# A decoder block on one core: the first two heads' k and q loaded at the end of the first part of the values' projection

## The chip, the core and the metric

The kernel runs on one core of a Trainium2 chip. The core has five engines that run side by side, each through its own instructions in order: TensorE (PE in the profile, with its weight loads as PEld), VectorE (DVE), ScalarE (ACT), GpSimd (POOL) and SyncE (SP), which here issues nearly all DMA transfers. They wait for each other through semaphores only. The metric is the time of one execution in microseconds (us), as the median of several runs. Lower is better.

## The reference

One transformer block on 1024 tokens of 1024 channels, in float32:

```python
h = rms_norm(x, g_pre_mix[l])
z = h @ w_in[l]
q, k, v, glu_in, z_ga, z_gc = jnp.split(z, ...)
y_attn = dilated_attention_mixer(q, k, v, rel_bias_table, w_attn_out[l])
y_conv = conformer_conv_mixer(glu_in, ...)
merged = jax.nn.sigmoid(z_ga) * y_attn + jax.nn.sigmoid(z_gc) * y_conv
x = x + rms_norm(merged @ w_mix_out[l], g_post_mix[l])
h = rms_norm(x, g_pre_ffn[l])
x = x + rms_norm(swiglu_ffn(h, w_ffn_in[l], w_ffn_out[l]), g_post_ffn[l])
```

The attention has 24 heads of 64 channels, in three groups of eight with dilations 1, 4 and 16. A query sees 128 steps of its dilation backwards, with a bias that depends on the distance. The three groups' outputs are merged per head slot, weighted by their softmax denominators. The convolution is causal and depthwise over 31 taps; a layer norm over the channels and a swish follow it.

## The kernel before

Float32 operands are split in a high and a low half, written as `fp32r`, and a product is made of two or three matmuls of these halves. The kernel is written out by hand: what Python calls in order is the order of each engine's queue.

**The order of the work.** Gated projections, gates and then all q and k are projected (`qk_pair`); k and q of each pair of heads are stored to DRAM. Then comes the stage around the change, the values' projection: six parts (`B.v`, L943, called at L1588), one for each of three groups and two halves of the heads. A part has eight columns of 128 tokens. A column is eight pairs of matmuls, L966 (128x512) and L967 (128x256), into one of six PSUM banks; then ScalarE copies the bank into half of the tile `vsum` (L977), and after every second column GpSimd adds the two halves of the tile up (L988). After columns 3 and 7 two stores take the sums to DRAM (L951 or L953), put five ticks later.

**Ticks.** Side work is spread over the matmuls by a counter. `tick` (L121) is called after every second pair of matmuls of the values' projection, so a column is 4 ticks and a part 32. A tick first does what `later` (L118) has planned for it, then, at every fourth tick, one weight piece, then one step of each background generator. I count ticks from the start of the first part.

**Weights of the parts.** A part has two raw tiles of weights, cut into four pieces. At tick 4 of a part the next part's raw tiles are asked for (L177), at tick 16 its pieces are queued, and at ticks 16, 20, 24 and 28 one piece each is made by ScalarE (cast, L201) and VectorE (subtraction, L202) into a tile of its own. These pieces are for the next part. Each of a part's four weight tiles is last used in its column 7, ticks 29 to 32.

**The convolution's norm** (`conv_norm`, L1294) runs as a background generator through the same ticks. It loads eight tiles of the convolution's output (L1301, four at the start, four at ticks 7 to 18), takes the mean off (L1318, VectorE), squares into a new tile (L1321, ScalarE) and adds the squares up (L1324, VectorE): seven additions, the last at tick 39. At tick 46 TensorE sums over the channels in sixteen small matmuls (L415), ScalarE and VectorE make the reciprocal root of it (L419 to L424), and at tick 53 TensorE spreads it over the partitions (L430). Then each of the eight tiles is scaled (L1336) and put through the swish (L1339).

**The attention** (`attention`, L999) is a generator of its own. Its first `next` calls `stack_load` five times, which loads k and q of the first two heads: two tiles for q's high and low halves of each head (L892, L893), one tile for k of each head (two loads each, L899) and the bias tile (L488): nine DMA issues on SP's queue and six tiles. It also plans two calls of `double` (L904), in each of which GpSimd copies half of q's columns from one half of the partitions to the other (L908, L909, four copies). Then it does nothing until `normed` is 9, which the norm sets at tick 83. From the end of the first part on it is stepped by `beat`, 2.52 times a tick. Its first products are the scores, L1082.

**Buffers.** The tiles of 128x1024 called `b` come from one pool of 42 (`NSLOT`, `slot`, L80): normalised input, weights, raw weights, convolution tiles, squares and the heads' k and q alike. When a new tile is asked for and none is free, the instruction that first writes it waits for the last use of the one that it takes over.

Of the kernel before, what the change touches and what calls it, by code (L numbers as in the profile page):

```python
# [62 lines left out]
class Build:  # L63
# [935 lines left out]
    def attention(self):  # L999

        live, s, total = {}, 0, 96
        order = [(g, 2 * hg + i) for hg in range(2) for g in range(3) for i in range(2)]
        nxt, cur, u, x, V = self.stacks(*order.pop(0)), None, 8, None, None
        for i in range(5):
            self.stack_load(nxt)
        for hf in range(2):
            self.later(22 + 5 * hf, lambda p=nxt, hf=hf: self.double(p, hf))
        second = self.stacks(*order.pop(0))

        def there():  # L1010
            return nxt[1] // 2 * 3 + nxt[0] < self.vn

        while s < total + self.LP:
            if s < total:
                if x is None and nxt and there():
                    x = self.values(*nxt[:2])
                if u == 8:
                    while self.normed < 9 or x is None:
                        if second and second[5] < min(5, self.normed - 6):
                            self.stack_load(second)  # L1020
                        if x is None and there():
                            x = self.values(*nxt[:2])
                        yield 0
                    cur, u, nxt, V = nxt, 0, None, []
                    self.ending = s == total - 8
                live[s] = a = {}
                self.att_s(a, cur, V, u)
                u += 1

                if u in (4, 5):  # L1030
                    if len(V) < 2:
                        V.append(self.value_parts(x, u - 4))
                    if u == 5:
                        x = None
                if u == 6 and cur[0] == 2:
                    self.other_stats(cur)
                if u in (6, 7) and nxt:
                    self.double(nxt, u - 6)
                if u == 8:
                    cur[2] = cur[3] = V = None  # L1040
                if u == 1:
                    if second:
                        nxt, second = second, None
                    elif order:
                        nxt = self.stacks(*order.pop(0))
                if nxt and nxt[5] < 5:
                    self.stack_load(nxt)
            if 0 <= s - 1 < total:
                self.att_e(live[s - 1])
            yield 0  # L1050
            done, self.added = self.added, None
            if done:
                next(done)
            if 0 <= s - self.LT < total:
                self.att_t(live, s - self.LT)
                yield 0
            for _ in done or ():
                pass
            done = None
            if 0 <= s - self.LP < total:  # L1060
                yield from self.att_p(live, s - self.LP)
            s += 1
        for _ in self.added:
            pass
        self.added = None
# [381 lines left out]
def build(ctx, tc, aps):  # L1447
    B = Build(ctx, tc, aps)
# [133 lines left out]
    att = B.attention()  # L1582

    B.vsum = B.slot()
    vs = list(vj.values()) + [late[:1] or co[:1]]
    B.later(20, lambda: next(att))
    for i, (g, hg) in enumerate(vj):
        B.v(g, hg, vs[i], vs[i + 1])  # L1588
        if i == 0:
            B.fine = att  # L1590
        elif i == 4:
            assert cn not in B.gens
            cs = []
            B.later(16, lambda: cs.append(B.bg(B.conv_split())))
# [18 lines left out]
    def gate_load(d, late=0):  # L1613
        c = B.slot()
        if late:
            B.later(late, lambda: nc.sync.dma_start(c, d))
        else:
            nc.sync.dma_start(c, d)
        return c

    nxt = gate_load(B.d_gc[0], 1)
    ws = {}

    for n, hf in [(n, hf) for hf in range(2) for n in range(3)] + [(n, hf) for n in range(3, 8) for hf in range(2)]:
        if hf == 0:
            ws[n] = B.weights(co[n])
            mg[n] = nxt
            nxt = gate_load(B.d_gc[n + 1]) if n < 7 else (gate_load(B.d_ga[0]), gate_load(B.d_gc[0]))
# [221 lines left out]
    for j in range(PLAIN, FT):  # L1850
        s = [None, None]
        p, odd = divmod(j, 2)
# [231 lines left out]
```

## Time and profile before

| | us |
|---|---|
| median of 3 runs | 1693.77 |
| lowest and highest run | 1693.01, 1693.94 |
| the profiled execution, its own time | 1696.67 |
| its span, first to last instruction | 1694.9 |
| TensorE busy | 1679.5 (99%) |
| VectorE busy | 1260.1 (74%) |
| ScalarE busy | 817.2 (48%) |
| GpSimd busy | 511.4 (30%) |
| first pair of the values' projection (L966) | at 549.4 |
| first scores of the attention (L1082) | at 620.0 |
| HBM traffic | 169 GB/s over the span |

A row of a timeline gives the start, the duration, the engine, the line, the operation, the output and inputs by the program's names, their shapes and a count; in brackets stands the idle time of the engine before it and what ended it. A row of waits names the waiting instruction, what it waited for, the sum in us, how often, and the longest. A row of a window gives, for each engine, the busy time and the count of instructions, then the granted share of TensorE's clock, the busy share of the DMA engines and the GB/s. TensorE's matmuls overlap, so their durations do not add up; the distance of their starts tells the rate.

### The profile page before, as it was taken

What the parts mean: (1) busy time and instruction counts of PE and PEld (TensorE: products, weight loads), DVE (VectorE), ACT (ScalarE), POOL (GpSimd) and SP (SyncE); (2) the same over time, 40 slices, a digit from 0 to 9 for tenths busy, and PEclk for the clock granted to TensorE, in tenths of its full rate; (3) what the DMA queues carried; (4) which work ended last, traced back from release to release, by engine and by line L of the source; (5) the groups of instructions that cost most, each with busy time, mean ns of one, the idle gap of its engine ahead of it and who ended that gap; (6) DMA issues with size and microseconds to landing.
All of it is one profiled execution on the core that took longest, in us unless ns stands there. A gap on an engine that the chain in (4) does not pass through costs nothing.

```text
span 1694.9 us, 23464 instructions
## 1 busy us (share of the span) xinstructions
PE 1679.5 (99%) x8167; PEld 1406.3 (83%) x8167; DVE 1260.1 (74%) x2209; ACT 817.2 (48%) x1599; POOL 511.4 (30%) x399
## 2 busy tenths in 40 slices
PE   9999999999999999999999999999999999999998
PEld 7788888888888789999888888888888888888886
DVE  6789988888999668778985845775665566677686
ACT  6344334434444478888812446633333333354453
POOL 0017777887886345665300400000000000000000
PEclk9999999999999999999999999999999999999999
DMA  4342433455566877789998622132223222494334
GB/s 167 113 178 88 149 124 131 149 198 178 170 170 174 267 250 233 221 239 245 323 271 315 218 88 100 44 130 94 93 103 121 94 93 95 174 376 126 107 124 155
DMA packets 162563, 283.36 MB, mean 167 GB/s; under 512 B 47249, under 2 KB 78988, under 8 KB 162444
## 3 DMA queue, kind: packets, MB, share of 16 engines
q1 hardware_dynamic: 161948, 281.42, 50.7%
q8 instruction: 64, 1.05, 0.3%
q14 instruction: 55, 0.45, 0.1%
q0 software_dynamic: 352, 0.18, 0.1%
q10 hardware_dynamic: 144, 0.26, 0.0%
HBM read 191.10 MB, written 95.42 MB: 169 GB/s over the span
## 4 chain that ended last, share of the span: by engine, by line
PE 50%; DMA 1%; ACT 0%; DVE 0%; issue 0%; DVEq 0%
PE p L1968 12%; PE p L336 7%; PE p L334 7%; PE p L335 7%; PE p L1697 5%; PE p L318 3%; PE p L320 3%; PE p L319 3%; DMA b<-dw 1%; PE p L1428 0%; PE p L1153 0%; DVE b L1635 0%; ACT b L1286 0%; PE p L1082 0%; ACT b L1434 0%
## 5 line engine op out<-in xcount | busy, mean ns | idle before, releaser
L334 PE MATMUL p<-b,b 128*128 128x512 f32 x1204 | 468.8, 389 | 0.5 <-ACT c L353 0.3
L335 PE MATMUL p<-b,b 128*128 128x512 f32 x1204 | 468.4, 389 | 0.0
L336 PE MATMUL p<-b,b 128*128 128x512 f32 x1204 | 468.4, 389 | 0.0
L334 PEld LDWEIGHTS p<-b,b 128*128 128x128 f32 x1204 | 226.0, 188 | 48.4 <-DVE c L862 1.0
L335 PEld LDWEIGHTS p<-b,b 128*128 128x128 f32 x1204 | 226.0, 188 | 47.0
L336 PEld LDWEIGHTS p<-b,b 128*128 128x128 f32 x1204 | 226.0, 188 | 47.0
L1968 PE MATMUL p<-b,b 128*128 128x512 f32 x924 | 209.6, 389 | 0.0
L1968 PEld LDWEIGHTS p<-b,b 128*128 128x128 f32 x924 | 173.4, 188 | 36.0
L708 DVE SCALAR_TENSOR_TENSOR p<-b,par,p 128x511 f32<-128x511 f32 (+14 forms) x232 | 163.3, 738 | 0.0
L966 PE MATMUL p<-b,b 128*128 128x512 f32 x384 | 146.2, 412 | 2.1 <-DVE b L202 2.1
L318 PE MATMUL p<-b,b 128*128 128x512 f32 x368 | 147.0, 399 | 0.0
L320 PE MATMUL p<-b,b 128*128 128x512 f32 x368 | 143.6, 390 | 0.0
L319 PE MATMUL p<-b,b 128*128 128x512 f32 x368 | 143.5, 390 | 0.0
L208 ACT CAST b<-d 128x1024 fp32r<-128x1024 f32 x86 | 90.4, 1051 | 105.2 <-POOL d L229 55.2
L209 POOL TENSOR_TENSOR b<-d,b 128x1024 fp32r<-128x1024 f32 x44 | 106.9, 2429 | 79.9 <-ACT b L208 72.5
L209 DVE TENSOR_TENSOR b<-d,b 128x1024 fp32r<-128x1024 f32 x42 | 51.3, 1221 | 101.0 <-ACT b L208 101.0
L1287 DVE TENSOR_TENSOR b<-b,b 128x512 fp32r<-128x512 f32 x133 | 92.4, 699 | 22.0 <-ACT b L1286 20.1
L967 PE MATMUL p<-b,b 128*128 128x256 f32 x384 | 108.6, 283 | 0.0
L1286 ACT CAST b<-b 128x512 fp32r<-128x512 f32 x133 | 82.1, 619 | 48.4 <-PE p L1968 18.7
L1095 ACT ACTIVATE c<-c,stat 128x128 f32<-128x128 f32 (+1 forms) x192 | 85.1, 447 | 13.6 <-DVE stat L1085 12.4
L1697 PE MATMUL p<-b,b 128*128 128x512 f32 x384 | 89.4, 391 | 0.0
L208 ACT CAST b<-b 128x1024 fp32r<-128x1024 f32 x47 | 49.5, 1052 | 77.5 <-POOL b L236 37.2
(233 smaller groups left out, 2913.1 us busy)
## 6 DMA issues: line engine op xcount, KB each, us to landing
b<-w_in SPq DMA_DIRECT2D x30, 512.0 KB, 4.7
dk<-c SPq DMA_DIRECT2D x48, 256.0 KB, 4.4
dq<-c SPq DMA_DIRECT2D x48, 256.0 KB, 3.7
b<-dq SPq DMA_DIRECT2D x48, 256.0 KB, 4.0
b<-dk SPq DMA_DIRECT2D x48, 256.0 KB, 7.8
b<-w_fi SPq DMA_DIRECT2D x24, 512.0 KB, 5.3
d<-w_in SPq DMA_DIRECT2D x23, 512.0 KB, 4.5
dqS<-c SPq DMA_DIRECT2D x44, 256.0 KB, 2.1
```

The source lines that it names most:

```text
L208: self.nc.scalar.copy(hi, x)
L209: self.wsplit.tensor_tensor(lo, x, f(hi), op=OP.subtract)
L318: nc.tensor.matmul(ps, hi[:, s], a, start=kt == 0, stop=False)
L319: nc.tensor.matmul(ps, hi[:, s], b, start=False, stop=False)
L320: nc.tensor.matmul(ps, lo[:, s], a, start=False, stop=kt == nk - 1)
L334: nc.tensor.matmul(ps, hi[:, s], a, start=first and kt == 0, stop=False, skip_group_check=True)
L335: nc.tensor.matmul(ps, hi[:, s], b, start=False, stop=False, skip_group_check=True)
L336: nc.tensor.matmul(ps, lo[:, s], a, start=False, stop=kt == 3, skip_group_check=True)
L708: nc.vector.scalar_tensor_tensor(A[i][:, j:], src[i][:, :H - j], w[i], A[i][:, j:], op0=OP.mult, op1=OP.add)
L966: nc.tensor.matmul(ps, a, w, start=kt == 0, stop=kt == KT - 1, skip_group_check=True)
L1697: nc.tensor.matmul(banks[tt][nh], st, wt[:, nh * H:(nh + 1) * H], start=bool(kt == 0 and a), stop=bool(kt == KT - 1 and b))
L1968: nc.tensor.matmul(acc[t], x, y, start=first and e == 0, stop=last and e == 2, skip_group_check=True)
```

## The change

The attention's first step moves from tick 20, inside the first part, to the end of the first part, tick 32, after all of that part's instructions. The two calls of `double` are planned 17 and 22 ticks after that step in place of 22 and 27, so that they fall on ticks 49 and 54 where they were on 42 and 47. No instruction is added or taken away.

```diff
@@ -1004,7 +1004,7 @@
         for i in range(5):
             self.stack_load(nxt)
         for hf in range(2):
-            self.later(22 + 5 * hf, lambda p=nxt, hf=hf: self.double(p, hf))
+            self.later(17 + 5 * hf, lambda p=nxt, hf=hf: self.double(p, hf))
         second = self.stacks(*order.pop(0))
 
         def there():
@@ -1583,10 +1583,10 @@
 
     B.vsum = B.slot()
     vs = list(vj.values()) + [late[:1] or co[:1]]
-    B.later(20, lambda: next(att))
     for i, (g, hg) in enumerate(vj):
         B.v(g, hg, vs[i], vs[i + 1])
         if i == 0:
+            next(att)
             B.fine = att
         elif i == 4:
             assert cn not in B.gens
```

## The prediction

> **What bounds the kernel now.** I read the page, then TensorE's waits, then windows and timelines around the start of the values' projection.
>
> ```profile
> span 1694.9 us, 23464 instructions
> PE 1679.5 (99%) x8167; PEld 1406.3 (83%) x8167; DVE 1260.1 (74%) x2209; ACT 817.2 (48%) x1599; POOL 511.4 (30%) x399
> ...
> PE p L966 <- DVE b L202: 2.1, 1, 2.1
> PE p L415 <- DVE b L1324: 1.3, 1, 1.3
> PE p L501 <- DVE eps_ln L444: 1.2, 1, 1.2
> ```
>
> TensorE sets the time: it is busy nearly throughout, and all its waits together are a few us. The two longest lie close together, at the start of the stage that the change touches. They are these:
>
> ```profile
> 578.11 0.50 PE L966 MATMUL p<-b,b 128*128 128x512 f32 x1 [2.12 <-DVE b L202]
> 587.31 2.96 PE L415 MATMUL p<-mean_col,b 128*128 128x1 f32 x16 [1.31 <-DVE b L1324]
> 597.27 1.03 PE L430 MATMUL p<-ident,rs 128*128 128x128 f32 x8
> ...
> 32.29 1.84 PE L415 MATMUL p<-mean_col,b 128*128 128x1 f32 x16
> ...
> 584.60:588.00 3.40, 2.09 (x15) 1.65 (x14) 2.55 (x2) 1.77 (x2) 3.28 (x3) 1.00 0.50 164
> 588.00:590.00 2.00, 2.00 (x12) 2.00 (x11) 0.00 (x0) 0.09 (x1) 1.82 (x4) 0.50 0.11 45
> 594.00:596.00 2.00, 2.00 (x11) 1.76 (x10) 1.42 (x1) 0.24 (x1) 1.14 (x1) 0.79 0.00 0
> ```
>
> The first wait is for the second part's last weight piece, the second for the sum of squares of the convolution's norm. In the windows (busy time and count of TensorE, its weight loads, VectorE, ScalarE, POOL; then clock, DMA share, GB/s) the granted clock behind the second stands at 0.50 from 588 until about 594.8. The 16 tiny products of L415 take 2.96 there and 1.84 at us 32. The line's pairs in the low stretch, beside a full stretch of equal length:
>
> ```profile
> 563.00:570.00 7.00, 7.00 (x21) 3.75 (x20) 1.00 1.02 359
> 590.27:597.27 7.00, 6.92 (x14) 3.57 (x14) 0.67 0.17 48
> ```
>
> At full clock a pair of L966 and L967 takes 0.35 us (7 us hold 20 whole ones); a tick, two pairs, 0.7. Between L415 and L430 lie 14 pairs, due in 4.9 us, taking 7.0.
>
> **Why TensorE waits there.** ScalarE and VectorE were late, and the rows say for what.
>
> ```profile
> ACT b L1321 <- PE p L967: 4.6, 1, 4.6
> ACT b L201 <- DVE b L1324: 1.9, 1, 1.9
> ...
> 566.07 0.62 ACT L201 CAST b<-b 128x512 fp32r<-128x512 f32 x1 [1.86 <-DVE b L1324]
> 566.59 0.58 ACT L977 COPY b<-p 128x512 f32<-128x512 f32 x1
> 571.79 1.06 ACT L1321 ACTIVATE b<-b 128x1024 f32<-128x1024 f32 x1 [4.61 <-PE p L967]
> 572.75 0.60 ACT L201 CAST b<-b 128x512 fp32r<-128x512 f32 x1
> 574.70 0.61 ACT L201 CAST b<-b 128x512 fp32r<-128x512 f32 x1
> ...
> 563.66 2.32 DVE L1324 TENSOR_TENSOR b<-b,b 128x1024 f32<-128x1024 f32 x1
> 567.33 1.22 DVE L1318 TENSOR_TENSOR b<-b,b 128x1024 f32<-128x1024 f32 x1
> 568.47 1.22 DVE L1324 TENSOR_TENSOR b<-b,b 128x1024 f32<-128x1024 f32 x1
> 573.39 0.69 DVE L202 TENSOR_TENSOR b<-b,b 128x512 fp32r<-128x512 f32 x1 [3.70 <-ACT b L201]
> 577.37 0.68 DVE L202 TENSOR_TENSOR b<-b,b 128x512 fp32r<-128x512 f32 x1
> 581.38 5.88 DVE L1324 TENSOR_TENSOR b<-b,b 128x1024 f32<-128x1024 f32 x3
> ```
>
> A square (L1321) reads a convolution block and writes a new tile. It computes with nothing of a matmul's, so waiting for L967 means waiting for its buffer, which held a weight tile of the first part. Counting live tiles of the 42 in the code at tick 20: normalised input 16, value sums 1, mean 1, convolution blocks 8, squares 2, first part's weights 4, raw weights 2, first weight piece 1: 35. The two heads' six tiles make 41, the second piece 42. From there each new tile waits for a release, and the first part's weights are released only by its last column of products, ticks 29 to 32. ScalarE works in order, so both later casts (L201) and their L202 stand behind the square.
>
> **The change, part by part.** First the load: nine DMA issues and six tiles move from tick 20 to tick 32. Between those ticks the program asks for three weight pieces and three squares; these now find six free buffers. At tick 32 the four weight tiles, both raw tiles and older squares are back; my count stays at 41 or below afterwards.
>
> *Weight piece.* The square that started at 571.79 can follow L977, which ends at 567.17: 4.6 sooner. The casts behind it and their L202 move along, and the last L202 ends near 573.4 in place of 578.05. The products need it at 578.11 - 2.12 = 575.99. So 2.12 go, with 2.5 us to spare.
>
> *Sum of squares.* From 573.39 to 587.26 VectorE works without a break: 13.87. Without the 3.70 in front this starts at 569.69 and ends at 583.56. TensorE reaches L415 at 587.31 - 1.31 - 2.12 = 583.88. So 1.31 go too, by 0.3 us; a little more if the 1.9 of L201 helps. The bounds: at best no wait, at worst the chain still ends at 587.26 and the second wait grows by what the first loses. I take none, since the data are no bound: the last convolution block was issued by 563.56 and such loads take 6.8 (below).
>
> *Clock.* The low stretch costs 2.96 - 1.84 = 1.12 in L415 and 7.0 - 4.9 = 2.1 behind it, 3.2 together. At us 32 L415 stood in the stream without an idle gap, and the clock stayed at 1.00:
>
> ```profile
> 31.65:35.06 3.41, 3.41 (x25) 3.10 (x24) 3.20 (x8) 0.27 (x1) 0.00 (x0) 1.00 0.01 2
> ```
>
> So products of L415 alone did not lower it; 1.31 idle beside them did. Bounds 0 and 3.2; I take 3.2.
>
> The Trainium skill, page "TensorE: Matmul & The Clock Gate", section on how HAM oscillation bites, asks only that TensorE have no idle gap over about 3.4 us. By that rule neither gap here lowers the clock, removing them would not restore it, and the sum would be 3.43. The trace disagrees: 1.31 idle stood before the fall.
>
> *Queues.* The load's cost, from rows:
>
> ```profile
> 561.07 2.49 SPq L1301 DMA_DIRECT2D b<-dconv  x4
> 566.14 4.36 SPq L899 DMA_DIRECT2D b<-dk  x4
> 571.20 0.38 SPq L488 DMA_DIRECT2D c<-rep  x1
> 572.44 2.33 SPq L951 DMA_DIRECT2D dv<-d  x2
> 578.08 2.64 SPq L177 DMA_DIRECT2D b<-w_v  x2
> ...
> b<-dconv SPq DMA_DIRECT2D x8, 512.0 KB, 6.8
> b<-w_v SPq DMA_DIRECT2D x4, 512.0 KB, 8.4
> ```
>
> On SP's queue the nine issues, some 8 us from 563.66 to 571.58, move behind the two stores L951. These wait for POOL's L988 at 563.33 to 564.90 (below) and so go out earlier, at about 565. The third part's weights (L177) are asked for at tick 36 and now stand behind the nine: from about 574, when the first part's weights are free, the nine end near 582 and L177 near 584.6, landing by 593 where they now land by 589. The third part starts at tick 64: L415 ends at 585.7, 18 ticks and L430 later it is about 599.4. The last of its four pieces is wanted by then, 1.3 us of cast and subtraction after landing. Cover is some 5 us, so I take nothing.
>
> Second, the doubling: twice four casts of 64 partitions on POOL, from ticks 42 and 47 (20 + 22, 20 + 27) to 49 and 54 (32 + 17, 32 + 22).
>
> ```profile
> 563.33 1.57 POOL L988 TENSOR_TENSOR d<-b 128x512 f32<-128x512 f32 x1 [4.36 <-ACT b L977]
> ...
> 586.24 1.49 POOL L908 CAST b<-b 64x512 fp32r<-64x512 f32 x1
> 591.80 0.65 POOL L909 CAST b<-b 64x512 fp32r<-64x512 f32 x1
> 593.87 1.27 POOL L988 TENSOR_TENSOR d<-b 128x512 f32<-128x512 f32 x1 [1.42 <-ACT b L977]
> ...
> L1082 PE MATMUL p<-b,b x384: 224/277/386, 620.0 to 839.5; 128*128 128x128 f32 x104, 128*128 128x256 f32 x88
> ```
>
> All eight hold POOL from 586.24 to 592.45. They are moved past one L988, that of tick 48, and stand before the one of tick 56. Tick 48 is reached near 587.1 (585.7 and two ticks), its L988 is done near 589, the casts near 595, and the L988 of tick 56, due near 593.5, can be held by 1.5 us. Behind it stands ScalarE's next L977, which empties a bank; TensorE has six banks, some 17 us of products, and does not see this. Attention's first scores (L1082) come at 620.0, shifted 613.4, so 18 us cover the casts. Beside the norm's VectorE work they may stretch two operations, as L1324 stretched from 1.22 to 2.32 beside POOL: 0 to 2.2 off the path. Cost nothing.
>
> **Sum.** 2.12 + 1.31 + 3.2 = 6.6. Later TensorE waits are too few to take it back. The profiled execution took 1696.67, 1.8 around its span; it becomes 1690.1, span 1688.3. The timed median stands 2.9 below the profiled time, so 1693.77 - 6.6 = **1687.2**.
>
> **The rivals.**
>
> *The low clock does not pay back.* Both waits go, but a window stays low because some idle is left beside L415, or the timed runs never had it: their 2.9 below the profile is near 3.2. For: the margin of 0.3. Against: three timed runs within 0.93 of each other. 3.43 are gained: 1690.3. The page's rule gives the same.
>
> *The wait only moves.* Squares still get buffers late, because buffers are handed out in another order than I count, or VectorE keeps its end at 587.26: TensorE then waits 3.4 at L415 and nothing is gained, 1693.8; half-way about 1691. For: VectorE has no pause after 573.39. Against: the 3.70 pause before it.
>
> *Slower: third weights late.* If the heads' last tile must wait for the last square sum, near 582.5, the nine issues end at 590.5, L177 at 593, landing 601.4; with cast and subtraction 1.3, the third part waits from 599.4 to 602.7, 3.3, and a low clock adds 3.2: the 6.5 eats the gain. From that point each us later is a loss; released only behind L415, at 585.7, it is 1693.8 - 6.6 + 6.5 + 3.2 = 1696.9. Against: four weight tiles are free by 574, before that sum.
>
> **How the numbers follow.** Forecast 0.54, its own range 1685.5 to 1688.8 (0.3 margin one way, small waits elsewhere the other). Low clock stays 0.20. Wait only moves 0.12. Slower 0.08. The remaining 0.06 is reassigned buffers later in the kernel, either sign. The range 1684.8 to 1692.6 takes in the first two and half of the third. About 0.2%, 3.4 us, is what a measurement can tell from no change: the forecast is faster, half of the second rival is, half of the rest, and some of the third: 0.72. Same 0.16, slower 0.12.
>
> **What would show it.** Right: no L1321 waiting for L967; L966 waits for L202 and L415 for L1324 gone; granted clock 1.00 from 580 to 600; first L1082 near 613. L951's first store near 565 and the nine loads behind it near 574. Wrong: L415 waiting longer than 1.31; the clock at 0.50 anyway; L966 waiting for L202 near 599 behind a late L177; L988 held behind casts that wait for a load.

## The result, and the profile after

| | before | after |
|---|---|---|
| median, us | 1694.28 (1693.01 to 1697.55, 13 runs) | 1690.26 (1689.25 to 1693.17, 13 runs) |
| ratio after / before, 95% interval | | 0.9977 (0.9968 to 0.9986) |
| the profiled execution, its own time and span | 1696.67, 1694.9 | 1690.83, 1689.0 |

The changed kernel is faster by 4.0 us, where 6.6 were forecast. The time lies in the range of 1684.8 to 1692.6, but outside the range of the forecast itself, 1685.5 to 1688.8; it is that of the first rival, "the low clock does not pay back" (3.43 gained, 1690.3). That the wide range held is owed to what it allowed for the rivals. Between the two profiled executions, however, lie 5.8 us. Much of what follows is about these two numbers.

First the page of the changed kernel and TensorE's waits: over the whole span, and behind the "...", at the head of a second list, from 545 to 640 us.

```profile
span 1689.0 us, 23464 instructions
PE 1676.4 (99%) x8167; PEld 1403.7 (83%) x8167; DVE 1259.8 (75%) x2209; ACT 818.9 (48%) x1599; POOL 513.4 (30%) x399
...
PE p L1082 <- DMA b<-dk: 1.3, 1, 1.3
PE p L501 <- DVE eps_ln L444: 1.2, 1, 1.2
PE p L1153 <- DVE c L1128: 1.0, 1, 1.0
...
PE p L334 <- DVE c L862: 0.2, 1, 0.2
PE p L1082 <- DVE stat L1085: 0.2, 1, 0.2
```

Both waits of the stage are gone. In the 95 us from 545 to 640 TensorE now waits 0.4. The three longest waits that are left lie elsewhere: in the attention's late blocks, near 811 and 818, and at the kernel's start (L501).

Next the timelines of ScalarE and VectorE. This execution reaches the first L966 0.6 us later than before's (550.0 against 549.4), so 0.6 is to be taken off a time before it is held against one of before.

```profile
566.52 1.06 ACT L1321 ACTIVATE b<-b 128x1024 f32<-128x1024 f32 x1
567.48 0.61 ACT L201 CAST b<-b 128x512 fp32r<-128x512 f32 x1
...
569.35 1.07 ACT L1321 ACTIVATE b<-b 128x1024 f32<-128x1024 f32 x1
570.32 0.61 ACT L201 CAST b<-b 128x512 fp32r<-128x512 f32 x1
...
573.32 0.68 DVE L202 TENSOR_TENSOR b<-b,b 128x512 fp32r<-128x512 f32 x1
...
577.33 5.90 DVE L1324 TENSOR_TENSOR b<-b,b 128x1024 f32<-128x1024 f32 x3
```

No square (L1321) has a bracket naming L967 any more; the one that started at 571.79 before starts at 566.52, right behind its L977. The last L202 ends at 574.00 where it ended at 578.05. The sum of squares ends at 583.23 (577.33 + 5.90) where it ended at 587.26.

TensorE's L415 comes at 584.16, with no idle time in front, 0.93 after the sum is done. The windows (the last three columns are granted clock, DMA share, GB/s) show the clock:

```profile
584.16 1.84 PE L415 MATMUL p<-mean_col,b 128*128 128x1 f32 x16
...
560.00:580.00 20.00, 20.00 (x115) 17.34 (x114) 18.03 (x16) 12.94 (x18) 4.99 (x3) 1.00 0.95 261
580.00:600.00 20.00, 20.00 (x124) 17.71 (x123) 12.82 (x15) 12.44 (x17) 12.45 (x11) 1.00 0.69 226
```

The sixteen products take the 1.84 of us 32, not the 2.96 at half clock. From the first L966 to the first L1082 lie 613.7 - 550.0 = 63.7 us, where before had 620.0 - 549.4 = 70.6. So 6.9 us went out of this stage in these two executions, and the span fell by 5.9.

The last view is of the queues: SP's, then POOL's, then the one row of ScalarE that answers to it.

```profile
565.49 0.88 SPq L951 DMA_DIRECT2D dv<-d  x2
572.34 0.52 SPq L892 DMA_DIRECT2D b<-dq  x1
...
577.69 0.58 SPq L488 DMA_DIRECT2D c<-rep  x1
578.37 0.89 SPq L177 DMA_DIRECT2D b<-w_v  x2
...
588.28 1.29 POOL L988 TENSOR_TENSOR d<-b 128x512 f32<-128x512 f32 x1 [6.14 <-ACT b L977]
589.63 0.95 POOL L908 CAST b<-b 64x512 fp32r<-64x512 f32 x1
...
591.32 0.61 POOL L908 CAST b<-b 64x512 fp32r<-64x512 f32 x1
...
596.96 1.49 POOL L909 CAST b<-b 64x512 fp32r<-64x512 f32 x1
598.54 2.15 POOL L988 TENSOR_TENSOR d<-b 128x512 f32<-128x512 f32 x1
...
600.72 0.59 ACT L977 COPY b<-p 128x512 f32<-128x512 f32 x1 [0.94 <-POOL d L988]
```

The nine loads run from 572.34 to 578.27, and L177 behind them is out by 579.26, 5 us before the time that the prediction gave it. The eight casts end at 598.45, some 3 us later than predicted: those that run beside VectorE's scaling (L1336, from 592.63) take 0.96 to 1.67 us in place of 0.61. The L988 behind them is late and ScalarE is held for 0.94. TensorE did not see it here.

### The profile page after: what moved, and what is told of

Same layout as the page of the kernel before. It is cut to its first block, busy times and chain, and to the rows that moved or that the text cites. A ratio compares the mean times of both kernels' runs of the same rounds, so it can differ in the third digit from the quotient of the medians.

```text
span 1689.0 us, 23464 instructions
## 1 busy us (share of the span) xinstructions
PE 1676.4 (99%) x8167; PEld 1403.7 (83%) x8167; DVE 1259.8 (75%) x2209; ACT 818.9 (48%) x1599; POOL 513.4 (30%) x399
## 4 chain that ended last, share of the span: by engine, by line
PE 93%; DMA 3%; DVE 1%; POOL 1%; issue 1%; ACT 1%; SPq 0%; DVEq 0%; ACTq 0%; POOLq 0%
PE p L334 15%; PE p L335 15%; PE p L336 15%; PE p L1968 12%; PE p L966 5%; PE p L1697 5%; PE p L318 5%; PE p L320 5%; PE p L319 5%; PE p L967 3%; PE p L1082 2%; PE p L1153 2%; PE p L578 2%; PE p L1120 2%; DMA b<-dact 1%
## 5 line engine op out<-in xcount | busy, mean ns | idle before, releaser
L966 PE MATMUL p<-b,b 128*128 128x512 f32 x384 | 144.1, 407 | 0.0
L967 PE MATMUL p<-b,b 128*128 128x256 f32 x384 | 107.7, 281 | 0.0
```

What stands on the lines that cost most here:

```text
L966: nc.tensor.matmul(ps, a, w, start=kt == 0, stop=kt == KT - 1, skip_group_check=True)
L967: nc.tensor.matmul(ps[:, 256:], b, w[:, :256], start=False, stop=kt == KT - 1, skip_group_check=True)
```

## The experiments

Three groups of kernels ran, e0 to e3, e4 to e7 and e8 to e11, each on one chip with the kernel before beside it; its medians there were 1695.16, 1694.96 and 1695.30. The ratios, with 95% intervals, are estimates against these runs and not the quotients of the medians; the two differ by up to 0.0012 (e5_tick28: 0.9964 and, by the medians, 0.9976). Two theories stood at the start. **Tiles**: the six tiles taken at tick 20 leave the square without a buffer, and all else follows. **Traffic or casts**: the early loads or the early doublings disturb the stage, and the buffers are incidental.

**e1_hold**: the changed kernel, but with six tiles taken at tick 20. The heads' loads stay behind tick 32 and get these tiles.

```diff
+    def reserve():
+        B.held = [B.slot(F32R) for _ in range(6)]
+        for x in B.held:
+            nc.gpsimd.memset(f(x)[0:1, :24], 0.0)
+
+    B.later(20, reserve)
...
-            a, b = self.slot(F32R), self.slot(F32R)
+            a, b = self.tile6(), self.tile6()
...
-            k = self.slot(F32R)
+            k = self.tile6()
```

> The six tiles of the first two heads are taken at tick 20, by six memsets of 24 elements on GpSimd, and loaded at tick 32 as after the change; the doublings stay on ticks 49 and 54. If the live tiles are the cause, the square waits for the first part's weight tile again (4 to 5 us), TensorE waits 2.1 us for the last weight piece and about 1.3 for the sum of squares, and the gain is gone: 1693.5 to 1695, ratio to before 0.9990 to 1.0005. If the place of the nine loads in SP's queue or of the doublings is the cause, the time stays that of the changed kernel, about 1690.3, ratio 0.9977.

Measured: 1694.40 (11 runs), ratio 0.9991 (0.9982 to 1.0). Its waits (five added lines shift the numbers: L971 is L966, L1326 the square L1321, L972 is L967):

```profile
PE p L971 <- DVE b L202: 2.1, 1, 2.1
...
ACT b L1326 <- PE p L972: 4.6, 1, 4.6
...
ACT b L201 <- DVE b L1329: 1.9, 1, 1.9
```

The square's 4.6, the 1.9 of the cast L201 for the addition L1324 (here L1329) and TensorE's 2.1 are back to the tenth, and the ratio's interval reaches 1.0. There is no wait at L415 in this execution, though; the section on the hardware takes that up. The free tiles also let the loads go out early again, at 566.85, so this kernel alone doesn't part tiles from traffic.

**e2_traffic**: the changed kernel with nine copies of 256 KB from DRAM to DRAM put on SP's queue at tick 20, and no tile taken.

```diff
+    scratch = B.dram.tile([576, 1024], F32, name="scratch")
+
+    def traffic():
+        for i in range(9):
+            src = B.d_qk[0, 0][i // 4 % 2]
+            r = i % 4 * 64
+            nc.sync.dma_start(scratch[i * 64:i * 64 + 64], src[r:r + 64])
+
+    B.later(20, traffic)
```

> The changed kernel with nine copies of 256 KB from DRAM to DRAM issued on SP at tick 20, where the loads stood before; they take no tile of the pool, and their result is not used. If the live tiles are the cause, neither wait of TensorE returns: 1690 to 1691, ratio 0.997 to 0.9985. If it was the nine loads' share of the DMA engines, the convolution tiles and the weights land late again and 2 to 3.4 us of waits return: 1693 to 1694.5.

Measured: 1694.68 (11 runs), ratio 0.9996 (0.9986 to 1.0006). A miss in the time: neither of the two waits is back, and yet the gain is gone. TensorE's list names a new one, at the first scores:

```profile
PE p L1082 <- DVE stat L1085: 2.1, 2, 1.7
```

The copies push the nine loads back to 574.85, their casts to 591.82, and so further into the scaling. The profiled execution took 1691.93 and is one of the three fastest of this kernel, with a mean clock of 0.999. Eight of the eleven runs have 0.998 or less, so in most of them the clock fell as well, at a place that no profile shows. Whether the copies or the late casts cost the time was open; e8 to e10 take it up.

**e3_doubles**: the kernel before, with only the doublings moved, to ticks 49 and 54.

```diff
-            self.later(22 + 5 * hf, lambda p=nxt, hf=hf: self.double(p, hf))
+            self.later(29 + 5 * hf, lambda p=nxt, hf=hf: self.double(p, hf))
```

> The kernel before with the doublings alone moved, from ticks 42 and 47 to 49 and 54 (the load stays at tick 20). If the live tiles are the cause, nothing changes: both waits of 2.1 and 1.3 us stay, ratio 0.9995 to 1.0005. If the doublings' place on GpSimd made the gain, 1690 to 1692.

Measured: 1695.24 (11 runs), ratio 1.0003 (0.9994 to 1.0012). Both waits stand, 2.1 and 1.3. The second half of the change does nothing by itself.

**e0_before** and **e4_after**: the two kernels again, for a second profile of each.

> The kernel before, once more, to see the granted clock of each run. If the low clock behind the second wait belongs to most executions, most runs have a mean clock of 0.997 and the runs at 0.999 are about 3 us faster than the rest. If it fell on the profiled execution by chance, most runs have 0.999 at 1693 to 1695 and the few at 0.997 lie near 1697.

> The changed kernel once more, beside the others on one chip, for the granted clock of each run. If the gain is the two waits of TensorE (2.1 and 1.3) and what the clock loses behind them, ratio 0.9970 to 0.9980, about 4 us below before, and nearly all runs at a mean clock of 0.999. If its first result owed anything to another chip, the ratio is above 0.9985.

Measured: e0_before 1695.37 (11 runs), ratio 1.0002 (0.9993 to 1.0011). e4_after 1692.33 (8 runs), ratio 0.9974 (0.9964 to 0.9984): the gain of the first comparison holds by this ratio, while the medians of that group lie only 2.6 us apart (1694.96 and 1692.33; quotient 0.9984). One of e0_before's eleven runs has a mean clock of 0.999, seven have 0.998 and three less, which is neither of the two cases of the expectation. Of e4_after's eight runs six have 0.999.

**e5_tick28**: the kernel before, with the load at tick 28 in place of 20 or 32 and the doublings at 49 and 54.

```diff
-            self.later(22 + 5 * hf, lambda p=nxt, hf=hf: self.double(p, hf))
+            self.later(21 + 5 * hf, lambda p=nxt, hf=hf: self.double(p, hf))
...
-    B.later(20, lambda: next(att))
+    B.later(28, lambda: next(att))
```

> The load at tick 28, four ticks earlier than in the changed kernel, the doublings on ticks 49 and 54. By the count of live tiles only the last weight piece and the last squares then wait, for weight tiles that are released at ticks 31 and 32, near 573: the piece is ready by 574.5, before it is needed at 576, so no first wait; the sum of squares ends about 1 us later than after the change, so the second wait is 0 to 0.8. Time 0 to 1.5 above the changed kernel, ratio to before 0.9975 to 0.9985. If any load before the end of the first part brings the loss back, 1694 to 1695.

Measured: 1690.92 (5 runs), ratio 0.9964 (0.9951 to 0.9978); neither wait is there. It is faster than expected, though not separable from the changed kernel. ScalarE's last weight cast does wait 3.35 for a tile of the first part (at 574.06), as the count had it, but TensorE does not see it. Tick 28 is late enough.

**e6_hold5**: as e1_hold, with five tiles held.

```diff
-        B.held = [B.slot(F32R) for _ in range(6)]
+        B.held = [B.slot(F32R) for _ in range(5)]
```

> As the run that held six tiles from tick 20, but five are held and the sixth is taken at tick 32. By the count the first tile that finds no buffer is then the third weight piece and no longer the square before it: it waits for the first part's first weight tile, near 572.4, the last piece is ready near 574.5 and TensorE's first wait (2.1) is gone, while the sum of squares ends only about 1 us sooner than before the change and the second wait is 1.5 to 2.5. Time 1692.5 to 1694.5, between the two kernels, and a lowered clock in most runs. If tiles do not matter, the time is that of the changed kernel; if any held tile brings everything back, both waits stand.

Measured: 1695.07 (11 runs), ratio 0.9995 (0.9987 to 1.0004). TensorE's list and ScalarE's (L1329 is the addition L1324):

```profile
PE p L415 <- DVE b L1329: 1.3, 1, 1.3
PE p L971 <- DVE b L202: 1.2, 1, 1.2
...
ACT b L201 <- PE p L972: 4.7, 1, 4.7
```

With one tile more to be had, the stall moves by one allocation. It is now the cast of the third of the four weight pieces that waits for a tile of the first part, not the square in front of it. TensorE's wait falls from 2.1 to 1.2. That the first wait would vanish and the second grow was a miss in the split, and the time is that of the kernel before, not between the two. The clock stayed at 1.00 through both waits:

```profile
586.00:588.00 2.00, 1.99 (x12) 1.51 (x10) 1.90 (x2) 0.00 (x0) 2.00 (x1) 1.00 1.01 399
588.00:590.00 2.00, 0.70 (x7) 0.71 (x7) 1.24 (x1) 1.79 (x2) 0.16 (x1) 1.00 0.36 117
```

**e7_tick40**: the load and the start of `beat` at tick 40, the doublings at 57 and 62.

```diff
+    def start_att():
+        next(att)
+        B.fine = att
+
...
-            next(att)
-            B.fine = att
+            B.later(8, start_att)
```

> The load eight ticks later than in the changed kernel, at tick 40, the doublings on ticks 57 and 62. If free tiles in ticks 20 to 32 are all that counts, the time is that of the changed kernel within 0.5 us: neither wait, the casts done near 600 for scores at 613. If there is still something to gain by keeping the nine loads away from the third part's weights, 1 us less; if the later casts, beside the norm's scaling on VectorE, hold the attention up, 1 to 3 us more.

Measured: 1696.80 (11 runs), ratio 1.0002 (0.9993 to 1.0011). Both waits are gone, and TensorE waits at the first scores instead, for L1085: 2.7 in all. It is the wait that e2 showed, larger.

**e8_casts42** and **e9_casts57**: the changed kernel, with only the doublings put at ticks 42 and 45, or at 57 and 62. **e10_traffic42**: e2_traffic with them at 42 and 45. **e11_tick28c42**: e5_tick28 with them at 42 and 45.

```diff
-            self.later(17 + 5 * hf, lambda p=nxt, hf=hf: self.double(p, hf))
+            self.later(10 + 3 * hf, lambda p=nxt, hf=hf: self.double(p, hf))
```

(In e9_casts57 it is 25 + 5 * hf, in e11_tick28c42 14 + 3 * hf.)

> The changed kernel with the doublings earlier, on ticks 42 and 45 (10 and 13 after the load). GpSimd is idle there between two additions, from about 582 to 588, and VectorE too, so the eight casts should take 0.6 each and hold no addition. If the casts beside the norm's scaling are what is left of the loss at the attention's start, ScalarE's 0.9 wait for GpSimd and TensorE's 0.2 to 0.5 wait at the first scores go: equal to the changed kernel or up to 1 us faster, ratio to before 0.9962 to 0.9978. If the loads have not landed by then, the casts hold the next addition and it is slower than that.

> The changed kernel, load at tick 32, with the doublings alone moved to ticks 57 and 62, where the run with the load at tick 40 had them. If the casts made that run slow (stretched to 1.5 each beside VectorE's scaling, holding the next addition, ScalarE's copy and the weight pieces behind it), TensorE waits 2 to 3 us at the first scores, the clock falls behind it, ratio 0.9990 to 1.0010. If the late load made it slow, this run is like the changed kernel, 0.9970 to 0.9980.

> The run with nine copies of traffic at tick 20, with its doublings on ticks 42 and 45. If traffic costs nothing by itself and that run lost its time by casts that came 2 us late, the gain is back: ratio 0.9965 to 0.9980. If the traffic costs by itself (third part's weights late), ratio 0.9990 to 1.0000 again.

> The load at tick 28 and the doublings on ticks 42 and 45: the most slack for the casts that still leaves the weight pieces their buffers. If both findings hold, no wait at the second part, none at the sum of squares beyond 0.5, none at the first scores: ratio 0.9958 to 0.9975, the fastest of all or equal to it.

| | load at tick | casts at ticks | copies | us | ratio |
|---|---|---|---|---|---|
| e8_casts42 | 32 | 42, 45 | no | 1691.94 | 0.9981 (0.9972 to 0.9990) |
| e9_casts57 | 32 | 57, 62 | no | 1693.08 | 0.9989 (0.9978 to 1.0) |
| e10_traffic42 | 32 | 42, 45 | yes | 1691.28 | 0.9979 (0.9971 to 0.9988) |
| e11_tick28c42 | 28 | 42, 45 | no | 1692.33 | 0.9981 (0.9972 to 0.9990) |

e10 holds as much traffic as e2 and keeps the gain, and the wait at the scores is down to 0.2, so by these two ratios e2's loss was that of its casts. The traffic is not quite free: in e10's profile the third part's weights land late, and TensorE waits 0.54 for the last piece made of them, a small case of the rival "third weights late" (e2's profile has no such wait):

```profile
590.04 0.62 ACT L201 CAST b<-b 128x512 fp32r<-128x512 f32 x1 [3.33 <-DMA b<-w_v]
...
602.76 0.50 PE L966 MATMUL p<-b,b 128*128 128x512 f32 x1 [0.54 <-DVE b L202]
```

e9 moves nothing but the casts, and brings the wait at the scores; the interval of its ratio overlaps that of the changed kernel and reaches 1.0. Whether the late casts make up all of e7's loss (ratio 1.0002) it does not show. Its timelines:

```profile
597.52 1.49 POOL L908 CAST b<-b 64x512 fp32r<-64x512 f32 x1
...
607.84 0.61 POOL L909 CAST b<-b 64x512 fp32r<-64x512 f32 x1
608.53 1.28 POOL L988 TENSOR_TENSOR d<-b 128x512 f32<-128x512 f32 x1
...
609.85 0.59 ACT L977 COPY b<-p 128x512 f32<-128x512 f32 x1 [2.81 <-POOL d L988]
...
614.95 0.59 ACT L977 COPY b<-p 128x512 f32<-128x512 f32 x1 [1.38 <-POOL d L988]
615.43 0.62 ACT L201 CAST b<-b 128x512 fp32r<-128x512 f32 x1
...
616.08 0.69 DVE L202 TENSOR_TENSOR b<-b,b 128x512 fp32r<-128x512 f32 x1 [8.78 <-ACT b L201]
616.69 0.28 DVE L1085 CUSTOM_DVE_ANT_0 c<-p,c 128x128 f32<-128x128 f32 x1
...
617.25 1.01 PE L1082 MATMUL p<-b,b 128*128 128x256 f32 x3 [2.64 <-DVE stat L1085]
```

Read downwards: the casts end 10.9 us after they began; L988 stands behind them on POOL; ScalarE's L977 waits for L988, first 2.81, then 1.38; the cast L201 stands behind L977; VectorE's L202 waits for L201, and the scores' own L1085 stands behind L202 in VectorE's order, though it needs nothing from it. TensorE's next scores need what L1085 frees. None of the four kernels beats the changed one beyond the intervals; that e8 might gain up to 1 us more and e11 be the fastest of all was not borne out.

## Why the prediction was right, and which term was off

**The buffers.** Right, and shown. Holding six tiles from tick 20 brings the square's 4.6 and the 2.1 back (e1); five move the stall by one allocation (e6); loading at tick 28 does without it (e5); moving the doublings alone (e3) gains nothing, and traffic with early casts (e10) keeps the gain, but for the 0.54 above. The rivals "the wait only moves" and "slower: third weights late" fell: L177 was out at 579.26, because the tiles came free with the first part's weights (SP's first load waits 5.9 us for L967), as the argument against that rival had it.

**The first wait, 2.12.** Gone as worked out: the last L202 ends at 574.0, 573.4 with the later start taken off, which is the time predicted.

**The second wait, 1.31.** Gone, with 0.93 to spare where 0.3 was predicted. The sum ended at 583.23; less 0.6 that is 582.6, a microsecond under the 583.56 of the prediction. It had named the 1.9 of L201 as a possible help and counted it at nothing. That wait is gone too, and e1 brings it back with the six tiles: it was the same lack of buffers, one allocation ahead of the square. The prediction's count is thus one tile short: it gave this cast, that of the second piece, the last free tile, and the trace has it wait for one.

**The casts.** At nothing, as predicted, but the estimate of "0 to 2.2 off the path" looked at VectorE's operations and not at the casts, which are stretched themselves. They end at 598.45, not near 595. The cover of 18 us that the prediction named, up to the first scores, was the wrong one to count: as e9 shows, what runs out first is the slack of POOL's next L988.

**The clock, 3.2: the mis-sized term.** The step was: "Bounds 0 and 3.2; I take 3.2". It was right for the execution that it was read from: 6.9 us went out of the stage between the two profiles, 6.6 were said, the windows of 560 to 600 stand at 1.00, and the profiled execution took 1690.83 where 1690.1 was worked out. But the kernel before doesn't always lose these 3.2. On the medians the term comes to 4.0 - 3.43 = 0.6, and the interval of the ratio (2.4 to 5.4 us) allows 0 to 2.0. The step rested on the sentence that 1.31 idle beside L415 lowered the clock; e6_hold5 has the same 1.31 before the same L415, at a clock of 1.00, so the gap alone doesn't decide. In the second profiled execution of before (e0_before) the clock fell somewhere else:

```profile
PE p L966 <- DVE b L202: 2.1, 1, 2.1
...
578.00:580.00 2.00, 1.13 (x5) 0.95 (x6) 2.00 (x4) 0.72 (x3) 0.00 (x0) 0.95 1.07 292
580.00:582.00 2.00, 2.00 (x8) 1.70 (x7) 2.00 (x2) 1.52 (x2) 0.41 (x1) 0.50 1.04 330
582.00:584.00 2.00, 2.00 (x10) 1.72 (x9) 2.00 (x2) 1.64 (x2) 1.37 (x1) 0.70 0.84 301
584.00:586.00 2.00, 2.00 (x14) 1.75 (x13) 1.79 (x3) 0.59 (x1) 1.05 (x1) 1.00 0.71 268
588.00:590.00 2.00, 2.00 (x20) 1.96 (x19) 0.02 (x1) 0.95 (x1) 1.82 (x4) 1.00 0.13 49
```

Here the clock is low right behind the first wait and back by 584. The missing clock sums to 2 x (0.05 + 0.50 + 0.30) = 1.7 us of work. TensorE, later by that much, found the sum of squares done: there is no wait at L415 (at 588.19, the sum done at 588.03) and no fall behind it. This execution lost 2.1 + 1.7 = 3.8 in the stage, the first one 6.6. From first L966 to first L1082 it is 617.7 - 550.2 = 67.5 us, against 70.6 and, after, 63.7.

The timed runs can be sorted by the mean granted clock that each lists. The fall at the kernel's end alone gives 0.999 (after's row 1680 to 1689 stands at 0.80: 9 x 0.20 = 1.8 us of 1689). A stretch of 3.4 us at 0.50 takes off another 1.7, or 0.001; one of 6.8 takes off 0.002.

| mean clock | 0.999 | 0.998 | 0.997 | 0.995, 0.996 |
|---|---|---|---|---|
| before, 90 runs beside the experiments: runs | 7 | 46 | 30 | 7 |
| their median, us | 1694.45 | 1694.44 | 1696.32 | |
| after, 21 runs (first comparison and e4_after): runs | 18 | 2 | 1 | |
| their median, us | 1690.83 | 1692.96 | 1693.17 | |

The profile of before, on which the sum was made, belongs to the 30 (0.997); more runs belong to the 46, which lie 1694.44 - 1690.83 = 3.6 us above most runs of after. This sum mixes chips; where both kernels ran on one, beside e4_after, it is 1694.22 - 1691.71 = 2.5. The mean also doesn't say where a stretch lay: in kept profiles of other kernels with 0.998 it was at the kernel's start (e6_hold5, e8_casts42) or near 815 (e5_tick28), and e1_hold's 0.997 comes from two short ones, near 582 and near 826. So the table fits the account, and does not prove it for the timed runs. What the two profiles show is that the term is not one number for all executions: 3.2 in the first, and in e0_before 1.7 in place of the second wait's 1.31, so 0.4 more. The first rival had the right price, and its second reason, that the timed runs never had the low stretch of the profile, fits this table for most of them; its first, that a stretch stays low after the change, does not. The prediction had the hint in hand, the timed median 2.9 below the profiled time, and took it as a fixed offset between the two.

The span of after also holds waits that do not belong to the change: at L1082 for k's load 1.3, 1.9 in e4_after, against 0 in before's first profile and 0.9 in e0_before. Whether the earlier attention adds to this wait these four executions can't tell.

## What to carry to other kernels

Before a load is put early, count the live buffers at that point; a prefetch whose buffers are taken before they are needed shows up elsewhere, as a wait of an unrelated write for the last reader of the buffer that it takes over. A loss that a granted clock adds is to be taken from more than one execution, or with 0 as its lower end, since the same gap may cost nothing in the next one. When work is moved on a side engine, look at what stands next in that engine's queue, not only at the moved work's own due time.

## What was unexpected in the hardware

**The clock fell after 1 to 2.6 us of idle time, and not every time.** The kernel before was, in e0_before, low for 3.4 us behind the gap of 2.1 near 578, or, in the first profile, at full clock there and low for 6.8 us behind the gap of 1.3 near 587. In e9_casts57 the gap of 2.64 at the first scores did it:

```profile
614.00:616.00 2.00, 0.61 (x5) 0.41 (x4) 0.00 (x0) 1.05 (x3) 0.92 (x1) 1.00 1.01 297
616.00:618.00 2.00, 0.75 (x3) 0.75 (x4) 1.80 (x9) 1.52 (x7) 1.38 (x2) 0.77 1.00 371
618.00:620.00 2.00, 2.00 (x10) 1.81 (x9) 1.35 (x5) 2.00 (x7) 1.92 (x3) 0.50 1.04 358
620.00:622.00 2.00, 2.00 (x15) 1.91 (x15) 1.72 (x8) 1.76 (x7) 1.92 (x2) 0.88 1.05 240
```

In e5_tick28 it fell behind a gap of 0.98 near 812, 0.4 us of idle time shortly ahead of it. In e6_hold5 gaps of 1.2 and 1.3 left it at 1.00, in e2_traffic one of 1.66 near 617, in e4_after one of 1.89 near 820. The Trainium skill, page "TensorE: Matmul & The Clock Gate", section on how HAM oscillation bites, puts the limit at a gap of about 3.4 us; these runs disagree, with falls behind 0.98 to 2.64. The same page's note on the warm-up speaks of a free-running window of activity of about 3.4 us that makes a kernel's cold stretch vary between runs; that would fit a fall that depends on where a gap lies, and the lengths of 3.4 and 6.8, but what decides in one execution was not tried.

**A low clock can pay for a later wait.** In e0_before and e1_hold the early fall made TensorE late enough for the sum of squares, and the wait of 1.3 vanished. Two losses of the kernel before the change are thus partly alternatives, not terms to be added.

**POOL's casts and VectorE's two-input operations stretch each other.** A cast of 64x512 takes 0.61 us alone and mostly 1.49 beside L1336 (up to 1.67); L1324 takes 1.22 alone and 2.32 beside L988 (the prediction's rows). The Trainium skill, page "SBUF — State Buffer", section "SBUF: two separate sides", has the two engines share a pair of ports that one operation holds for its whole length when VectorE's has two inputs there; the stretched rows on both sides fit that. In e8_casts42, where the casts lie in the pause ahead of the scaling, six of eight take 0.61. That this gained nothing over the changed kernel, as e11 gained nothing over e5, stays unexplained on the medians. e8_casts42's own profile has a wait of 1.8 at the kernel's start (L578), whose cause was not followed, and one of 1.31 at the third group of scores, behind the same stretching at another place:

```profile
619.31 1.29 POOL L940 TENSOR_TENSOR b<-b,b 128x512 fp32r<-128x512 f32 x1
...
619.32 1.83 DVE L202 TENSOR_TENSOR b<-b,b 128x512 fp32r<-128x512 f32 x1 [0.62 <-ACT b L201]
...
621.89 0.74 PE L1082 MATMUL p<-b,b 128*128 128x256 f32 x4 [1.31 <-DVE stat L1085]
```

L202 takes 1.83 in place of 0.69 beside GpSimd's subtraction L940, and L1085, for which TensorE waits, stands behind it.
